# Half of a opens in two half-row parts, and a late turn of a stands one place earlier, in a fused matmul, GELU, matmul kernel

## The chip, the cores and the metric

The kernel runs on one NeuronCore of a Trainium2 chip. The metric is the device time of one execution in microseconds (us). Shown times are medians of several executions; a profile is of one execution, whose own time is given beside its span.

## The reference

```python
m, k, n, p = 1024, 1024, 2048, 1024            # a: m x k, b: k x n, c: n x p, all float32

def reference(a, b, c):
    h = np.matmul(a, b)
    h = 0.5 * h * (1 + np.tanh(np.sqrt(2 / np.pi) * (h + 0.044715 * h ** 3)))
    return np.matmul(h, c).astype(np.float32)
```

## The kernel before

All of the work is laid out by hand: the order in which instructions are written is the order in which each engine takes them, and semaphores that the framework derives from the tiles order the engines against each other. Both matrix products are cut into two by two blocks of 512 rows or columns and use seven block products where that helps; nothing from line 231 on differs in the change, so only the opening is described.

The opening computes the first half of the transposed hidden layer's upper part, `h11`: eight tiles of 128 columns of b (index t) by the first 512 rows of a. Each tile sums over eight slices of 128 of the inner dimension (index k, `KT` = 8, `KH` = 4). A product in this stage is one TensorE matmul of 128 by 512 (`mm0`, L151): the weights are a tile of b's slice k in bf16 (`b_lo`), the moving side is `aT[0][:, k, :]`, the transposed a. The sums lie in PSUM banks: `ps[0]` to `ps[5]` come from the pool `ppool` (six banks), `ps[6]` and `ps[7]` from `tpool` (two banks).

**Loads.** The SP queue loads a's first half as four tiles of 128 full rows (`load_a0`, L70, 512 KB each) and then b's left half slice by slice (`load_b0`, L77, 512 KB each, six buffers). POOL loads the other half of a (`a1`, L181) and then the rest of b, the later slices and c. It starts behind a small copy of b's slice 4 (`gate`, L86), and `a1` takes the same four buffers that `ab` held.

**Turning a.** Each tile mt of a is cast to bf16 in two halves of 512 columns (`cast_a0`: g = 0 on DVE at L103, g = 1 on ACT at L105). Four TensorE transposes turn a half (`turn0`, L113) into a PSUM bank. A copy takes it to `aT[0]` (`copy0`: DVE at L119, ACT at L121). One half covers slices 0 to 3 or 4 to 7. Before the first product of the opening, both halves of tiles 0, 1 and 2 are turned, and the first half of tile 3; the second half of tile 3 is turned amid slice 0 (L156). Each turn writes a bank of its own: two of `tpool` in rotation, and two of `ppool` (`side`) for tile 2. Products of zeros (`warm_up`, L95) fill TensorE between the turns.

**Casting b.** `cast_b0(k)` casts a slice of b to bf16, half on ACT (L130) and half on DVE (L132), one slice ahead of the products.

**Products.** Slices 0 to 3 run over seven tiles, slices 4 to 7 over six; tile 6 then takes its last four slices and tile 7 all eight. Between the two halves of tile 7 stand the first two late turns of a (`turn(0)`, `turn(1)`: eight transposes at L191, a DVE copy at L192 and an ACT copy at L193 each). The other two late turns follow the first half-width product (`mm1_half`, eight products of 128 by 256, L198). GELU on ACT (L169) empties the banks.

Of the kernel before, what the change touches and what calls it, by code (L numbers as in the profile page):

```python
# [9 lines left out]
F32 = mybir.dt.float32  # L10
BF16 = mybir.dt.bfloat16
# [3 lines left out]
AF = mybir.ActivationFunctionType  # L15
# [4 lines left out]
def kernel(ctx, tc, a, b, c, out):  # L20
    nc = tc.nc
    M, K = a.shape
    _, N = b.shape
    _, P = c.shape
    KT = K // 128
    NT = N // 128
    MT = M // 128
    H = 512
    N0 = 6
    W0 = N // 2  # L30
    KH = KT // 2
    NH = NT // 2
    R = range(4)

    av = a.rearrange("(mt p) k -> p mt k", p=128)
    bv = b.rearrange("(kt p) n -> p kt n", p=128)
# [5 lines left out]
    astage = ctx.enter_context(tc.tile_pool(name="astage", bufs=4))  # L42
    abf = ctx.enter_context(tc.tile_pool(name="abf", bufs=4))
    b0stage = ctx.enter_context(tc.tile_pool(name="b0stage", bufs=6))
    opool = ctx.enter_context(tc.tile_pool(name="opool", bufs=4))
    ppool = ctx.enter_context(tc.tile_pool(name="ppool", bufs=6, space=PSUM))
    tpool = ctx.enter_context(tc.tile_pool(name="tpool", bufs=2, space=PSUM))

    warm = consts.tile([128, H], BF16, name="warm")
# [11 lines left out]
                               for g in range(2)] for h in range(2)]  # L61


    a_st, b_st = {}, {}

    def load_a0(mt, parts):
        st = astage.tile([128, K], F32, name="a_st")
        w = K // parts
        for i in range(parts):
            nc.sync.dma_start(out=st[:, ts(i, w)], in_=av[:, mt, ts(i, w)])  # L70
        a_st[mt] = st

    def load_b0(k, parts):
        st = b0stage.tile([128, W0], F32, name="b0_st")
        w = W0 // parts
        for i in range(parts):
            nc.sync.dma_start(out=st[:, ts(i, w)], in_=bv[:, k, ts(i, w)])  # L77
        b_st[k] = st

    gate = consts.tile([128, 1], F32, name="gate")  # L80
    for mt in R:
        load_a0(mt, 1)
    for k in range(KT):
        load_b0(k, 1)

    nc.gpsimd.tensor_copy(gate, b_st[4][:, 0:1])  # L86
    g = consts.tile([128, 1], F32, name="g")
    nc.scalar.activation(g, warm[:, 0:1], AF.Gelu_apprx_tanh)

    side = [ppool.tile([128, 8, 128], BF16, name="ps", tag="ps") for _ in range(2)]  # L90
    ps = [ppool.tile([128, H], F32, name="ps", tag="ps") for _ in range(4)]

    def warm_up(n):
        for _ in range(n):
            nc.tensor.matmul(ps[3], warm[:, 0:128], warm, start=True, stop=True)  # L95

    warm_up(8)
    ab = []

    def cast_a0(mt, g):  # L100
        if g == 0:
            ab.append(abf.tile([128, K], BF16, name="ab1"))
            nc.vector.tensor_copy(ab[mt][:, 0:512], a_st[mt][:, 0:512])  # L103
        else:
            nc.scalar.activation(ab[mt][:, 512:K], a_st[mt][:, 512:K], AF.Copy)  # L105

    def turn0(mt, g):
        if mt == 2:
            pt = side[g]
        else:  # L110
            pt = tpool.tile([128, 8, 128], BF16, name="pt", tag="pt")
        for k in range(4):
            nc.tensor.transpose(pt[:, k, :], ab[mt][:, ts(4 * g + k, 128)], ident)  # L113
        return pt

    def copy0(mt, g, pt):
        dst = aT[0][:, ts(g, 4), ts(mt, 128)]
        if g == 0:
            nc.vector.tensor_copy(dst, pt[:, 0:4, :])  # L119
        else:  # L120
            nc.scalar.activation(dst, pt[:, 0:4, :], AF.Copy)  # L121

    HW = W0 // 2

    def cast_b0(k):
        v = {0: ((HW, W0),), 1: ((0, 256), (256, HW))}.get(k, ((0, HW),))
        a = {0: ((0, 256), (256, HW))}.get(k, ((HW, W0),))
        for i in range(max(len(v), len(a))):
            if i < len(a):
                nc.scalar.activation(b_lo[:, k, slice(*a[i])], b_st[k][:, slice(*a[i])], AF.Copy)  # L130
            if i < len(v):
                nc.vector.tensor_copy(b_lo[:, k, slice(*v[i])], b_st[k][:, slice(*v[i])])  # L132

    for mt in range(3):
        cast_a0(mt, 0)
        cast_a0(mt, 1)
        pt = [turn0(mt, 0), turn0(mt, 1)]
        if mt == 2:
            cast_a0(3, 0)
        copy0(mt, 0, pt[0])  # L140
        copy0(mt, 1, pt[1])
        warm_up((3, 6, 2)[mt])
    copy0(3, 0, turn0(3, 0))
    warm_up(2)
    ps += [ppool.tile([128, H], F32, name="ps", tag="ps") for _ in range(2)]
    cast_b0(0)
    cast_a0(3, 1)

    def mm0(t, ks):
        for k in ks:  # L150
            nc.tensor.matmul(ps[t], b_lo[:, k, ts(t, 128)], aT[0][:, k, :],  # L151
                             start=(k == 0), stop=(k == KT - 1))

    for t in range(N0):
        mm0(t, (0,))
    pt = turn0(3, 1)  # L156
    ps.append(tpool.tile([128, H], F32, name="pt", tag="pt"))
    mm0(6, (0,))
    cast_b0(1)
    copy0(3, 1, pt)  # L160
    ps.append(tpool.tile([128, H], F32, name="pt", tag="pt"))
    for k in range(1, KT):
        if k + 1 < KT:
            cast_b0(k + 1)
        for t in range(N0 + 1 if k < 4 else N0):
            mm0(t, (k,))

    def gelu(dst, src):
        nc.scalar.activation(dst, src, AF.Gelu_apprx_tanh)  # L169

    def bank(w=H):
        return ppool.tile([128, w], F32, name="ps", tag="ps", padded_shape=[128, H])
# [6 lines left out]
    for j in R:  # L179
        st = abf.tile([128, K], BF16, name="ab1")  # L180
# [7 lines left out]
    def turn(j):  # L188
        pt = ppool.tile([128, KT, 128], BF16, name="ps", tag="ps")
        for k in range(KT):  # L190
            nc.tensor.transpose(pt[:, k, :], a1[j][:, ts(k, 128)], ident)  # L191
        nc.vector.tensor_copy(aT[1][:, :, ts(j, 128)], pt)  # L192
        nc.scalar.activation(a22[:, :, ts(j, 128)], aT[1][:, KH:KT, ts(j, 128)], AF.Copy)  # L193

    def mm1_half(t, q):
        p = bank(256)
        for k in range(KT):
            nc.tensor.matmul(p, b_lo[:, k, ts(t, 128)], aT[1][:, k, ts(q, 256)],  # L198
                             start=(k == 0), stop=(k == KT - 1))
        gelu(h21[:, t, ts(q, 256)], p)  # L200
# [5 lines left out]
                             start=(k == 0), stop=(k == KT - 1))  # L206
        gelu(dst, p)

    mm0(6, range(4, KT))
    gelu(h11[:, 6, :], ps[6])  # L210
    mm0(7, range(4))
    turn(0)
    turn(1)
    mm0(7, range(4, KT))
    gelu(h11[:, 7, :], ps[7])
    mm1_half(0, 0)
    turn(2)
    turn(3)
    mm1_half(1, 0)
    mm1_half(2, 0)  # L220
# [77 lines left out]
    for j in R:  # L298
        p = bank()
        prod(p, KH, whole(bx), whole(aT[0]), j)  # L300
        nc.scalar.activation(v2[:, j, :], p, AF.Copy)
    for j in R:
        p = bank()
# [4 lines left out]
    for j in R:  # L308
        p = bank()
# [8 lines left out]
    for j in R:  # L318
        p = bank()
# [10 lines left out]
    for j in R:  # L330
        p = bank()
# [5 lines left out]
    for j in R:  # L337
        p = bank()
# [24 lines left out]
    for j in R:  # L363
        p = bank()
# [29 lines left out]
    for j in R:  # L394
        p = bank()
# [4 lines left out]
    for j in R:  # L400
        p = bank()
# [5 lines left out]
    for j in R:  # L407
        p = bank()
# [8 lines left out]
    for j in R:  # L417
        p = bank()
# [3 lines left out]
    for j in R:  # L422
        p = bank()
        prod(p, NH, halves(s2), whole(c22), j)
        combine(j, 1, p, p5[:, j, :])
    for j in R:
        p = bank()
        prod(p, NH, whole(h22), pairs(t2), j)
        combine(4 + j, 0, p, u3[j])
    for j in range(3):  # L430
        p = bank()
        prod(p, NH, whole(h12), whole(c21), j)
        combine(j, 0, p, p1[:, j, :])
    for q0, w, queue in ((0, 256, nc.sync), (256, 128, nc.scalar), (384, 128, nc.sync)):
        p = bank(w)
# [33 lines left out]
```

## Time and profile before

| What | Value |
|---|---|
| median of 8 runs | 121.01 us (120.39 to 121.19) |
| profiled execution, its own time | 120.5 us |
| its span | 118.7 us |
| TensorE busy with products | 113.9 us (96%) |
| DVE busy | 81.9 us (69%) |
| ACT busy | 46.3 us (39%) |
| POOL busy | 26.6 us (22%) |
| TensorE clock granted, mean | 0.999 |

The span runs from the first to the last instruction; the execution's own time is 1.8 us longer, for what lies around it. Busy time is the union of an engine's instructions; TensorE's is counted with overlapping, pipelined matmuls, so 96% does not say that each of them runs at its best rate. In lines of the timeline the first number is the start in us, the second the time from the first start to the last end of a merged group, then engine, line, operation, what it writes and reads, its shape and how many; in brackets stands the engine's idle time before it and what ended that.

### The profile page before, as it was taken

What the parts mean: (1) busy time and instruction counts of PE and PEld (TensorE: products, weight loads), DVE (VectorE), ACT (ScalarE), POOL (GpSimd) and SP (SyncE); (2) the same over time, 40 slices, a digit from 0 to 9 for tenths busy, and PEclk for the clock granted to TensorE, in tenths of its full rate; (3) what the DMA queues carried; (4) which work ended last, traced back from release to release, by engine and by line L of the source; (5) the groups of instructions that cost most, each with busy time, mean ns of one, the idle gap of its engine ahead of it and who ended that gap; (6) DMA issues with size and microseconds to landing.
All of it is one profiled execution on the core that took longest, in us unless ns stands there. A gap on an engine that the chain in (4) does not pass through costs nothing.

```text
span 118.7 us, 1596 instructions
## 1 busy us (share of the span) xinstructions
PE 113.9 (96%) x583; PEld 76.4 (64%) x589; DVE 81.9 (69%) x112; ACT 46.3 (39%) x78; POOL 26.6 (22%) x39
## 2 busy tenths in 40 slices
PE   5999999999999999999999999999999999999990
PEld 2554444469744445888887447888888888886460
DVE  0344322048999917999999999995789992824450
ACT  5366744987332474306369998430000000000000
POOL 2000069752200000086305229100006500000000
PEclk9999999999999999999999999999999999999999
DMA  3999999999999999949999999999997999954434
GB/s 115 407 384 282 420 420 223 180 359 386 213 211 203 206 206 375 359 113 247 250 235 202 190 196 200 182 204 148 141 163 159 243 266 342 344 197 160 175 116 151
DMA packets 13543, 28.41 MB, mean 239 GB/s; under 512 B 992, under 2 KB 5472, under 8 KB 13536
## 3 DMA queue, kind: packets, MB, share of 16 engines
q0 software_dynamic: 9216, 17.83, 73.0%
q1 hardware_dynamic: 4176, 10.42, 23.5%
q8 instruction: 4, 0.07, 0.2%
q10 hardware_dynamic: 144, 0.07, 0.2%
q14 instruction: 3, 0.02, 0.1%
HBM read 20.97 MB, written 4.19 MB: 212 GB/s over the span
## 4 chain that ended last, share of the span: by engine, by line
PE 94%; DVE 2%; ACT 1%; issue 1%
PE ps L267 63%; PE ps L151 9%; PE ps L205 7%; PE ps L198 5%; PE ps L95 4%; PE pt L151 2%; PE pt L113 1%; PE ps L191 1%; DVE aT L192 1%; ACT aT L121 1%; ACT ab L105 0%; PE ps L113 0%; DVE aT L119 0%; DVE ot L438 0%; DVE warm L50 0%
## 5 line engine op out<-in xcount | busy, mean ns | idle before, releaser
L267 PE MATMUL ps<-t,s 128*128 128x512 f32 x64 | 14.9, 392 | 0.0
L267 PE MATMUL ps<-c,h 128*128 128x512 bf16 (+2 forms) x78 | 14.1, 336 | 0.1
L267 PEld LDWEIGHTS ps<-t,s 128*128 128x128 f32 x64 | 12.0, 188 | 2.6
L275 DVE TENSOR_TENSOR ot<-ps,v 128x512 f32<-128x512 f32 x16 | 10.5, 695 | 3.1 <-PE ps L267 3.1
L169 ACT ACTIVATE h<-ot 128x512 bf16<-128x512 f32 (+1 forms) x16 | 9.4, 624 | 5.9 <-DVE ot L275 5.9
L267 PE MATMUL ps<-t,h 128*128 128x512 f32 x48 | 11.7, 389 | 0.0
L267 PEld LDWEIGHTS <-h 128*128 128x128 bf16 x80 | 7.1, 98 | 7.0 <-issue 0.5
L169 ACT ACTIVATE h<-ps 128x512 bf16<-128x512 f32 (+2 forms) x17 | 8.3, 528 | 8.2 <-PE ps L205 5.9
L383 DVE TENSOR_TENSOR ot<-ps,p 128x512 f32<-128x512 f32 x11 | 7.5, 689 | 5.5 <-PE ps L267 3.1
L151 PE MATMUL ps<-aT,b_lo 128*128 128x512 bf16 x46 | 11.1, 379 | 0.2
L151 PEld LDWEIGHTS <-b_lo 128*128 128x128 bf16 x64 | 6.1, 98 | 7.6 <-DVE b_lo L132 0.6
L267 PEld LDWEIGHTS ps<-t,h 128*128 128x128 f32 x48 | 9.0, 188 | 1.9
L205 PE MATMUL ps<-aT,b_lo 128*128 128x512 bf16 x39 | 8.7, 379 | 0.1
L95 PE MATMUL ps<-warm 128*128 128x512 bf16 x21 | 7.3, 485 | 1.2 <-DVE warm L50 1.2
L132 DVE CAST b_lo<-b_st 128x512 bf16<-128x512 f32 (+1 forms) x9 | 3.5, 396 | 6.3 <-DMA b_st<-in_b_dram 6.3
L267 PE MATMUL ps<-as,bt 128*128 128x512 f32 x32 | 7.7, 396 | 0.0
L285 POOL DMA_DIRECT2D c<-in_c_dram x8 | 6.4, 838 | 5.6 <-DMA b<-in_b_dram 3.9
L267 PE MATMUL ps<-c,s 128*128 128x512 f32 x32 | 7.4, 389 | 0.0
L267 PE MATMUL ps<-as,b 128*128 128x512 f32 x32 | 7.4, 389 | 0.0
L267 PE MATMUL ps<-aT,bx 128*128 128x512 bf16 x31 | 7.0, 379 | 0.1
L416 POOL DMA_DIRECT2D t<-c x4 | 3.5, 1041 | 15.5 <-PE ps L267 14.5
L267 PEld LDWEIGHTS ps<-as,bt 128*128 128x128 f32 x32 | 6.0, 188 | 1.4
(71 smaller groups left out, 171.5 us busy)
## 6 DMA issues: line engine op xcount, KB each, us to landing
b_st<-in_b_dram SPq DMA_DIRECT2D x8, 512.0 KB, 9.0
out_dram<-ot SPq DMA_DIRECT2D x15, 256.0 KB, 2.1
c<-in_c_dram POOLq DMA_DIRECT2D x6, 512.0 KB, 18.1
t<-c POOLq DMA_DIRECT2D x6, 512.0 KB, 6.6
a_st<-in_a_dram SPq DMA_DIRECT2D x4, 512.0 KB, 4.6
b<-in_b_dram POOLq DMA_DIRECT2D x2, 1024.0 KB, 10.4
c<-in_c_dram POOLq DMA_DIRECT2D x2, 1024.0 KB, 21.0
t<-t POOLq DMA_DIRECT2D x4, 512.0 KB, 8.6
```

Of the source, the lines that this page charges most:

```text
L95: nc.tensor.matmul(ps[3], warm[:, 0:128], warm, start=True, stop=True)
L113: nc.tensor.transpose(pt[:, k, :], ab[mt][:, ts(4 * g + k, 128)], ident)
L132: nc.vector.tensor_copy(b_lo[:, k, slice(*v[i])], b_st[k][:, slice(*v[i])])
L151: nc.tensor.matmul(ps[t], b_lo[:, k, ts(t, 128)], aT[0][:, k, :], start=(k == 0), stop=(k == KT - 1))
L169: nc.scalar.activation(dst, src, AF.Gelu_apprx_tanh)
L198: nc.tensor.matmul(p, b_lo[:, k, ts(t, 128)], aT[1][:, k, ts(q, 256)], start=(k == 0), stop=(k == KT - 1))
L205: nc.tensor.matmul(p, b_lo[:, k, ts(t, 128)], aT[h][:, k, :], start=(k == 0), stop=(k == KT - 1))
L267: nc.tensor.matmul(p, lhs(t)[:, ts(j, 128)], rhs(t)[:, q], start=(t == 0), stop=(t == n - 1))
L275: tt(ot, p, u, op=ADD)
L285: nc.gpsimd.dma_start(out=dst[:, t:t + 4, :], in_=cv[:, r * NH + t:r * NH + t + 4, ts(q, H)])
L383: tt(ot, p, u, op=ADD)
L416: nc.gpsimd.dma_start(out=t2[i], in_=c21[:, P2[i], :], accum_op=ADD)
```

## The change

The four tiles of a's first half are now loaded in half rows: 256 KB each for slices 0 to 3 first, then b's slices 0 to 3, then the other half rows, then b's slices 4 to 7. Only the first halves of the four tiles are cast, turned and copied ahead of the first product, each into the bank of a later sum (`ps[0]` to `ps[3]`), with the work divided anew between DVE and ACT. The second halves are cast behind the casts of slice 3, those of tiles 2 and 3 later between the copies; tile 0's is turned amid slice 3, after its fourth product, and those of tiles 1, 2 and 3 between slice 3 and slice 4. All four second-half turns write `ps[7]`, which is cut into two halves that they use in turn. Slices 4 to 7 then run over seven tiles like the first four, so tile 6 is done with them and tile 7 alone follows. Warm-up products go into `ps[5]`, and are 8 + 2 + 2 + 2 + 4. Last, `turn(2)` stands ahead of the GELU of tile 7 and of the first half-width product, where it stood behind it.

```diff
-    def load_a0(mt, parts):
-        st = astage.tile([128, K], F32, name="a_st")
...
+    def load_a0(g):
+        for mt in R:
+            nc.sync.dma_start(out=a_st[mt][:, ts(g, H)], in_=av[:, mt, ts(g, H)])
...
-    for mt in R:
-        load_a0(mt, 1)
-    for k in range(KT):
-        load_b0(k, 1)
+    for g in range(2):
+        load_a0(g)
+        for k in range(g * KH, g * KH + KH):
+            load_b0(k)
...
-    side = [ppool.tile([128, 8, 128], BF16, name="ps", tag="ps") for _ in range(2)]
-    ps = [ppool.tile([128, H], F32, name="ps", tag="ps") for _ in range(4)]
+    ps = [ppool.tile([128, H], F32, name="ps", tag="ps") for _ in range(N0)]
+    ps += [tpool.tile([128, H], F32, name="pt", tag="pt") for _ in range(2)]
...
+    def turned(mt, g):
         if g == 0:
+            return ps[mt][:, :].bitcast(BF16)[:, 0:512].rearrange("p (k m) -> p k m", k=4)
+        return ps[7][:, :].bitcast(BF16)[:, ts(mt % 2, 512)].rearrange("p (k m) -> p k m", k=4)
...
-    for mt in range(3):
-        cast_a0(mt, 0)
-        cast_a0(mt, 1)
-        pt = [turn0(mt, 0), turn0(mt, 1)]
-        if mt == 2:
-            cast_a0(3, 0)
-        copy0(mt, 0, pt[0])
-        copy0(mt, 1, pt[1])
-        warm_up((3, 6, 2)[mt])
-    copy0(3, 0, turn0(3, 0))
+    cast_a0(0, 0, True)
+    turn0(0, 0)
     warm_up(2)
+    cast_a0(1, 0, False)
+    copy0(0, 0, True)
+    turn0(1, 0)
+    warm_up(2)
+    cast_a0(2, 0, True)
+    copy0(1, 0, False)
+    turn0(2, 0)
+    warm_up(2)
+    cast_a0(3, 0, True)
+    copy0(2, 0, False)
+    turn0(3, 0)
+    warm_up(4)
+    copy0(3, 0, True)
     cast_b0(0)
-    cast_a0(3, 1)
...
-    for t in range(N0):
-        mm0(t, (0,))
-    pt = turn0(3, 1)
-    ps.append(tpool.tile([128, H], F32, name="pt", tag="pt"))
-    mm0(6, (0,))
-    cast_b0(1)
-    copy0(3, 1, pt)
-    ps.append(tpool.tile([128, H], F32, name="pt", tag="pt"))
-    for k in range(1, KT):
-        if k + 1 < KT:
+    for k in range(KH):
+        if k + 1 < KH:
             cast_b0(k + 1)
-        for t in range(N0 + 1 if k < 4 else N0):
+        else:
+            cast_a0(0, 1, True)
+            cast_a0(1, 1, False)
+        for t in range(7):
+            mm0(t, (k,))
+            if k + 1 == KH and t == 3:
+                turn0(0, 1)
+                copy0(0, 1, True)
+    turn0(1, 1)
+    copy0(1, 1, False)
+    cast_a0(2, 1, True)
+    turn0(2, 1)
+    cast_a0(3, 1, True)
+    copy0(2, 1, False)
+    turn0(3, 1)
+    copy0(3, 1, True)
+    for k in range(KH, KT):
+        cast_b0(k)
+        for t in range(7):
             mm0(t, (k,))
...
-    mm0(6, range(4, KT))
     gelu(h11[:, 6, :], ps[6])
-    mm0(7, range(4))
+    mm0(7, range(KH))
     turn(0)
     turn(1)
-    mm0(7, range(4, KT))
+    mm0(7, range(KH, KT))
+    turn(2)
     gelu(h11[:, 7, :], ps[7])
     mm1_half(0, 0)
-    turn(2)
     turn(3)
```

The last argument of `cast_a0` and `copy0` is the engine: True is DVE, False ACT.

More of the change, by code (lines that the diff above doesn't have):

```diff
@@ L61, with load_b0 @@
                                for g in range(2)] for h in range(2)]
-    a_st, b_st = {}, {}
-    def load_a0(mt, parts):
-        st = astage.tile([128, K], F32, name="a_st")
[L68 to L78, printed above, removed]
+    a_st = [astage.tile([128, K], F32, name="a_st") for _ in R]
+    b_st = {}
+    def load_a0(g):
+        for mt in R:
+            nc.sync.dma_start(out=a_st[mt][:, ts(g, H)], in_=av[:, mt, ts(g, H)])
+    def load_b0(k):
+        b_st[k] = b0stage.tile([128, W0], F32, name="b0_st")
+        nc.sync.dma_start(out=b_st[k], in_=bv[:, k, 0:W0])
     gate = consts.tile([128, 1], F32, name="gate")
-    for mt in R:
-        load_a0(mt, 1)
-    for k in range(KT):
-        load_b0(k, 1)
+    for g in range(2):
+        load_a0(g)
+        for k in range(g * KH, g * KH + KH):
+            load_b0(k)
     nc.gpsimd.tensor_copy(gate, b_st[4][:, 0:1])
@@ L88, with cast_a0, copy0 @@
     nc.scalar.activation(g, warm[:, 0:1], AF.Gelu_apprx_tanh)
-    side = [ppool.tile([128, 8, 128], BF16, name="ps", tag="ps") for _ in range(2)]
-    ps = [ppool.tile([128, H], F32, name="ps", tag="ps") for _ in range(4)]
+    ps = [ppool.tile([128, H], F32, name="ps", tag="ps") for _ in range(N0)]
+    ps += [tpool.tile([128, H], F32, name="pt", tag="pt") for _ in range(2)]
     def warm_up(n):
         for _ in range(n):
-            nc.tensor.matmul(ps[3], warm[:, 0:128], warm, start=True, stop=True)
+            nc.tensor.matmul(ps[5], warm[:, 0:128], warm, start=True, stop=True)
     warm_up(8)
-    ab = []
-    def cast_a0(mt, g):
+    ab = [abf.tile([128, K], BF16, name="ab1") for _ in R]
+    def turned(mt, g):
         if g == 0:
-            ab.append(abf.tile([128, K], BF16, name="ab1"))
-            nc.vector.tensor_copy(ab[mt][:, 0:512], a_st[mt][:, 0:512])
+            return ps[mt][:, :].bitcast(BF16)[:, 0:512].rearrange("p (k m) -> p k m", k=4)
+        return ps[7][:, :].bitcast(BF16)[:, ts(mt % 2, 512)].rearrange("p (k m) -> p k m", k=4)
+    def cast_a0(mt, g, vector):
+        if vector:
+            nc.vector.tensor_copy(ab[mt][:, ts(g, H)], a_st[mt][:, ts(g, H)])
         else:
-            nc.scalar.activation(ab[mt][:, 512:K], a_st[mt][:, 512:K], AF.Copy)
+            nc.scalar.activation(ab[mt][:, ts(g, H)], a_st[mt][:, ts(g, H)], AF.Copy)
     def turn0(mt, g):
-        if mt == 2:
-            pt = side[g]
-        else:
-            pt = tpool.tile([128, 8, 128], BF16, name="pt", tag="pt")
+        pt = turned(mt, g)
         for k in range(4):
             nc.tensor.transpose(pt[:, k, :], ab[mt][:, ts(4 * g + k, 128)], ident)
-        return pt
-    def copy0(mt, g, pt):
+    def copy0(mt, g, vector):
         dst = aT[0][:, ts(g, 4), ts(mt, 128)]
-        if g == 0:
-            nc.vector.tensor_copy(dst, pt[:, 0:4, :])
+        if vector:
+            nc.vector.tensor_copy(dst, turned(mt, g))
         else:
-            nc.scalar.activation(dst, pt[:, 0:4, :], AF.Copy)
+            nc.scalar.activation(dst, turned(mt, g), AF.Copy)
     HW = W0 // 2
@@ L132, in cast_b0 @@
                 nc.vector.tensor_copy(b_lo[:, k, slice(*v[i])], b_st[k][:, slice(*v[i])])
-    for mt in range(3):
-        cast_a0(mt, 0)
-        cast_a0(mt, 1)
-        pt = [turn0(mt, 0), turn0(mt, 1)]
-        if mt == 2:
-            cast_a0(3, 0)
-        copy0(mt, 0, pt[0])
-        copy0(mt, 1, pt[1])
-        warm_up((3, 6, 2)[mt])
-    copy0(3, 0, turn0(3, 0))
-    warm_up(2)
-    ps += [ppool.tile([128, H], F32, name="ps", tag="ps") for _ in range(2)]
+    cast_a0(0, 0, True)
+    turn0(0, 0)
+    warm_up(2)
+    cast_a0(1, 0, False)
[11 more added lines that the diff above has]
+    copy0(3, 0, True)
     cast_b0(0)
-    cast_a0(3, 1)
     def mm0(t, ks):
```

## The prediction

> **What bounds the kernel now.** I read the chain of waits first, then the timeline up to 28 us in order of time, because the change touches nothing later.
>
> ```profile
> ## 4 chain that ended last, share of the span: by engine, by line
> PE 94%; DVE 2%; ACT 1%; issue 1%
> PE ps L267 63%; PE ps L151 9%; PE ps L205 7%; PE ps L198 5%; PE ps L95 4%; PE pt L151 2%; PE pt L113 1%; PE ps L191 1%; DVE aT L192 1%; ACT aT L121 1%; ACT ab L105 0%; PE ps L113 0%; DVE aT L119 0%; DVE ot L438 0%; DVE warm L50 0%
> ```
>
> TensorE carries the end nearly throughout: a microsecond of TensorE idleness in the opening moves the end by a microsecond, unless a later idle takes it back. So I need two things: when the first product (L151) starts, and how densely TensorE runs from there.
>
> ```profile
> 4.00 0.43 DVE L103 CAST ab<-a_st 128x512 bf16<-128x512 f32 x1 [2.87 <-DMA a_st<-in_a_dram]
> 6.85 0.40 PE L113 MATMUL pt<-ident,ab 128*128 128x128 bf16 x4 [0.17 <-ACT ab L105]
> 7.28 0.60 ACT L121 ACTIVATE aT<-pt 128x512 bf16<-128x512 bf16 x1 [0.49 <-PE pt L113]
> 8.04 0.43 DVE L103 CAST ab<-a_st 128x512 bf16<-128x512 f32 x1 [0.56 <-DMA a_st<-in_a_dram]
> 9.25 0.39 PE L113 MATMUL pt<-ident,ab 128*128 128x128 bf16 x4
> 9.68 0.43 DVE L119 COPY aT<-pt 128x512 bf16<-128x512 bf16 x1 [0.45 <-PE pt L113]
> 10.15 1.46 PE L151 MATMUL ps<-aT,b_lo 128*128 128x512 bf16 x5
> 11.70 0.50 DVE L132 CAST b_lo<-b_st 128x256 bf16<-128x256 f32 x2 [1.27 <-DMA b_st<-in_b_dram]
> ```
>
> Rows of a land from 4.0 to 8.0 us, 1.3 us apart; the last is cast, turned, copied, and L151 begins at 10.15. A turn (four transposes) until the end of its copy takes 0.86 us on DVE (9.25 to 10.11) and 1.03 us on ACT (6.85 to 7.88). Both serve as prices below.
>
> ```profile
> 12.05 1.47 PE L151 MATMUL ps<-aT,b_lo 128*128 128x512 bf16 x6
> 16.60 5.34 PE L151 MATMUL ps<-aT,b_lo 128*128 128x512 bf16 x23
> 21.78 1.89 PE L151 MATMUL pt<-aT,b_lo 128*128 128x512 bf16 x8
> 24.40 1.03 PE L151 MATMUL pt<-aT,b_lo 128*128 128x512 bf16 x4
> 25.50 1.05 PE L198 MATMUL ps<-aT,b_lo 128*128 128x256 bf16 x8
> 27.27 4.53 PE L198 MATMUL ps<-aT,b_lo 128*128 128x256 bf16 x40
> ```
>
> From 12.05 the products follow at 0.2155 us each (24 from 16.60 to 21.78); L198's half-width ones take 0.108, and a transpose 0.056 (16 of L191 between 23.50 and 24.40). Idle from 10.15 to 27.27 is about 0.4 us: 0.17 before 12.05, where b's second slice is late, and 0.24 before 25.50, where L198 waits for L192 (the six products from 10.15 to the turn at 11.45 fill 1.30 without a gap; one record is missing). I take 27.27, the start of half-width tile 1, as the milestone.
>
> **What the Trainium skill says.** "PSUM — Partial Sum Buffer", section on bank collisions, says to guard PSUM by bank and not by address, since two engines may not touch a bank's partitions together. The kernel before, with a bank for each turn, shows no such wait; the new code puts four turns into one bank. "TensorE: Matmul & The Clock Gate", Part 1, says that full clock comes only after a busy window of about 3.4 us that runs freely, and is lost after an idle one. The trace agrees on the first half: L95's first eight products fill 3.4 us from 1.19, 0.43 each, and six from 7.08 start 0.215 apart. No run here shows the loss. "DMA: Bandwidth & Descriptors", Anatomy, gives about 2 us fixed to a transfer; the first 512 KB of a, issued at 0.74, landed at 4.00, of which 1.28 is data at the spacing of later slices, so 1.98: agreed.
>
> **Part 1: half rows first.** SP issues four 256 KB half rows of a, b's slices 0 to 3, the other four half rows, then b 4 to 7: 16 issues for 12, each about 0.45 us, less than the 0.64 us of data of a half. Four more fixed costs in a pipelined queue cost nothing. The queue's 2 KB packets of output take 86 ns where the 4 KB ones of a take 159, so a half lands every 0.69 us: at about 3.4, 4.1, 4.8, 5.5, and b's slice 0 at 6.8 to 7.0. Ahead of b slice 4 stand the same 4.5 MB as before, so that slice and POOL's gate (L86), behind which all loads of a's second half are queued, stay near 15.6 us at the latest.
>
> With half the turns, TensorE's own order sets the start: eight warm-ups to 4.58 as now; four cold transposes to 5.00, two cold warm-ups to 5.86, then three turns (0.28 in the first case, else 0.22) with two warm-ups (0.43) between, ending at 7.46, and four warm-ups (0.86): 8.32. The last opening copy runs 7.66 to 8.09 and b's first cast on ACT 7.5 to 7.9, both under those warm-ups. So the first product starts at S = 8.32 against 10.15, **1.8 us earlier**. Before, DMA hid part of a late clock rise; in the new order all is TensorE, so S can be 8.3 to 9.5. I take 8.35 against the profiled rise.
>
> **Part 2: the other half, amid the products.** Slices 0 to 2 take 3 x 7 x 0.2155 = 4.53, four products of slice 3 take 0.86; the first second-half turn starts at T = S + 5.39 = 13.7. By then its half row has landed (about 11.5; 12.5 if the slow delivery of b's slice 1, 2.4 us instead of 1.28, recurs). Casts of the half rows on DVE and ACT stand behind casts of slice 3; DVE has 0.9 us of work for every 1.5 of TensorE, so they hide.
>
> The four turns then share bank ps[7], and the built program's list of waits has each turn waiting for the copy of the one before: turn 1 for DVE's copy 0, turn 2 for ACT's copy 1, turn 3 for ACT's copy 2; the last copy, on DVE, comes ahead of DVE's cast of b slice 4, for which the first product of slice 4 waits. Counted from T:
> - copy 0 (DVE) ends 0.86; three products of slice 3 cover TensorE to 0.87; turn 1 starts 0.90 (0.04 for a wait).
> - its copy on ACT ends 0.90 + 1.03 = 1.93; turn 2 starts 1.98, copy ends 3.01; turn 3 starts 3.06, DVE's copy ends 3.92.
> - DVE's cast of slice 4, which overlaps by 0.09 (9.68, then 10.02 in the trace), ends 4.26; slice 4 starts at 4.30.
>
> So TensorE stands from 0.87 to 4.30, 3.43 us, with 12 transposes (0.67) of its own: **2.76 us idle**, where the kernel before had one turn, 0.22 us, with six products around it. Nothing covers this: the remaining products all need all four quarters of aT, and tile 7 has no free bank until the turns are done. ACT's half of slice 4 is cast by T + 3.7, hidden.
>
> **Part 3: after it.** Slices 4 to 7 at seven tiles: 28 x 0.2155 = 6.03; tile 7's first four 0.86; 16 transposes 0.90; its last four 0.86; turn(2), now here, 0.45; half-width tile 0 0.86; turn(3) 0.45. The milestone is at T + 4.30 + 10.41 = S + 20.10 = 28.45, against 27.27: **+1.18 us**. Moving turn(2) ahead adds no work; it covers L198's wait of 0.24, already in this count. On ACT the copy of turn(2) now stands before tile 7's gelu; the banks that later work needs are freed by gelus ahead of it, and the 0.6 us hide. Its load lands at about 23.9 now and would be needed at 26.7. POOL's four loads reuse the buffers of ab and wait for the turns; the last waits for turn 3 at T + 3.3 = 17.0, while now it goes out at about 18.1: no delay. SP's late slices 6 and 7 may share the engines with POOL's loads about a microsecond earlier; slice 7 would land by 20 and is needed at 22.6.
>
> **What takes it back later?** Nothing that I find: DVE's sums L244 to L254 shift with it and have 4.8 us in hand:
>
> ```profile
> 39.78 2.36 DVE L254 TENSOR_TENSOR bt<-b,b 128x1024 fp32r<-128x1024 f32 x2
> 46.99 7.65 PE L267 MATMUL ps<-as,bt 128*128 128x512 f32 x32
> ```
>
> **Sum.** -1.80 (start) -0.41 (old idles) +2.76 (new idle) +0.67 (12 transposes more amid the products) is +1.22, or +1.18 by the milestone: +1.2. The profiled execution took 120.5 (span 118.7); it would be 121.7. The median, 121.01, lies 0.5 above it, which I read as a later clock rise or a slower slice of b; to the median the sum gives 122.2, and 0.1 is added for the new start's exposure to the clock: **122.3 us**.
>
> **Unknown costs.** The clock phase at the start: between nothing and +1.2 on S, against a part of that in the kernel before; I take +0.1. The slow slice of b: its recurrence costs nothing (b's slice 1 is needed at 9.8 and would land by 9.5), and if it held the kernel before in typical runs, its removal gives up to 0.5 back. The ACT copies of a shared bank: 0.57 to 0.63 each, plus or minus 0.1 over two.
>
> **Rivals.**
> - *The clock falls back* (8%). The 3.43 us hold only transposes, about one window of the skill's 3.4. If it counts as idle, products go at 0.43 for a window, 8 to 16 of them: +1.7 to 3.4. The time would be about 124.2. Against it: three bursts of work fall inside, and the window must align.
> - *The start gains less* (14%). b's slice 0 lands late or the rise comes at 8 us: S near 9.2, the time 123.0.
> - *A slow slice held the median run before* (14%): the new order is free of it; +0.7, 121.7.
> - *The turns do not wait for each other* (4%, faster). If the chain of copies at ps[7] were short, with turns back to back and both engines copying at once, slice 4 would start at T + 2.55 instead of T + 4.30, and the sum be 1.2 - 1.75 = -0.55: 120.5. It decides from T + 3.1 downward, where the gain of the start outweighs the gap. Against it stand the program's waits named above and the 1.03 us of each ACT turn.
> - *No difference to be seen* (6%): half of that shortening and a slow slice gone.
>
> **How the numbers follow.** The forecast itself has 54% and its own range is 121.9 to 122.7. The late start, slow slice and clock add above and below: 121.4 to 123.7 leaves out the faster and equal cases and half of the clock's. Within 0.3% (0.36 us), about what a measurement here can tell from no change: faster 0.04, same 0.06, slower 0.90.
>
> **What would show it.** Right: the first product (line 149 in the new file) near 8.3 to 8.5; a wall of about 3.4 us between slices 3 and 4, near 14.6 to 18.0, with three bursts of four transposes, each released by a copy of the turn before; then no idle before the half-width tiles and the same work after them, 1.2 us later. Wrong: the first product after 9, turns released by their own casts only, or 0.43 us spacing after the gap.

## The result and the profile after

The changed kernel took **124.16 us** in the median (123.22 to 125.77, 11 executions) against 121.06 for the kernel before on the same chip: a ratio of 1.0242, 95% interval 1.0217 to 1.0266, or +2.9 us (the two medians lie 3.1 apart). Forecast were 122.3 us and a range up to 123.7. The direction was right, the size less than half of what came. The profiled execution took 123.22 us with a span of 121.4, which is 2.7 above the span before. Executions that stood apart by over 1.5% are left out of ratios, not out of medians.

The chain of waits of the changed kernel, on its page:

```profile
## 4 chain that ended last, share of the span: by engine, by line
PE 87%; DMA 5%; ACT 1%; SPq 1%; DVE 1%; issue 1%
PE ps L274 62%; PE ps L149 9%; PE ps L213 7%; DMA b_st<-in_b_dram 5%; PE ps L206 4%; PE pt L149 3%; PE ps L199 1%; SPq L69 1%; ACT aT L116 1%; PE pt L109 1%; DVE b_lo L127 1%; ACT b_lo L125 0%; DVE aT L114 0%; DVE ot L445 0%
```

TensorE's share fell from 94 to 87%. A transfer of b, which was not on the chain before, now carries 5% of the span: at the start the chain runs through SP's issues and b's slice 0, where it ran through warm-up products and turns.

From the timeline up to the first product (start, duration, engine, line, what; in brackets the idle time before and what ended it):

```profile
3.39 0.43 DVE L102 CAST ab<-a_st 128x512 bf16<-128x512 f32 x1 [2.25 <-DMA a_st<-in_a_dram]
5.07 0.63 ACT L104 ACTIVATE ab<-a_st 128x512 bf16<-128x512 f32 x1 [2.83 <-DMA a_st<-in_a_dram]
5.74 0.43 DVE L102 CAST ab<-a_st 128x512 bf16<-128x512 f32 x1 [0.27 <-DMA a_st<-in_a_dram]
6.40 0.43 DVE L102 CAST ab<-a_st 128x512 bf16<-128x512 f32 x1 [0.24 <-DMA a_st<-in_a_dram]
7.30 1.03 PE L89 MATMUL ps<-warm 128*128 128x512 bf16 x4
9.01 0.43 DVE L127 CAST b_lo<-b_st 128x512 bf16<-128x512 f32 x1 [1.09 <-DMA b_st<-in_b_dram]
9.48 1.47 PE L149 MATMUL ps<-aT,b_lo 128*128 128x512 bf16 x6 [1.16 <-DVE b_lo L127]
```

The first half row came at 3.4 as forecast. The second came 1.67 us behind it and not 0.69; b's slice 0 landed at 8.98, 2.6 us behind the last half row and not 1.3. TensorE's own order held: its last warm-ups ended at 8.33, as forecast. Then it stood for 1.16 us until slice 0 was cast, so the first product stands at 9.48, where 8.35 was forecast. In e2, e4 and e5 below, which load in the same way, it stands at 9.97, 9.67 and 9.80.

The gap between slices 3 and 4:

```profile
14.89 0.39 PE L109 MATMUL pt<-ident,ab 128*128 128x128 bf16 x4
15.31 0.42 DVE L114 COPY aT<-pt 128x512 bf16<-128x512 bf16 x1 [1.24 <-PE pt L109]
15.79 0.38 PE L109 MATMUL pt<-ident,ab 128*128 128x128 bf16 x4
16.21 0.60 ACT L116 ACTIVATE aT<-pt 128x512 bf16<-128x512 bf16 x1 [1.26 <-PE pt L109]
16.86 0.38 PE L109 MATMUL pt<-ident,ab 128*128 128x128 bf16 x4 [0.69 <-ACT aT L116]
17.28 0.60 ACT L116 ACTIVATE aT<-pt 128x512 bf16<-128x512 bf16 x1 [0.47 <-PE pt L109]
17.93 0.38 PE L109 MATMUL pt<-ident,ab 128*128 128x128 bf16 x4 [0.69 <-ACT aT L116]
18.43 0.42 DVE L114 COPY aT<-pt 128x512 bf16<-128x512 bf16 x1 [2.02 <-ACT b_lo L125]
19.24 1.47 PE L149 MATMUL ps<-aT,b_lo 128*128 128x512 bf16 x6 [0.93 <-DVE b_lo L127]
```

Each turn starts when the copy of the one before has ended; where ACT copies, a link takes 1.07 us. From the first turn to slice 4 it is 4.35 us (4.30 forecast). After it TensorE is dense again, and the half-width tile 1 starts at 29.68, 20.20 us behind the first product (20.10 forecast) and 2.41 us later than in the kernel before:

```profile
27.92 0.61 PE L199 MATMUL ps<-ident,ab 128*128 128x128 bf16 x8
28.36 1.04 PE L206 MATMUL ps<-aT,b_lo 128*128 128x256 bf16 x8
29.24 0.61 PE L199 MATMUL ps<-ident,ab 128*128 128x128 bf16 x8
29.68 4.53 PE L206 MATMUL ps<-aT,b_lo 128*128 128x256 bf16 x40
```

The last TensorE work of the program also ends 2.40 us later (118.12 against 115.72 on the chain in order of time), so between the milestone and the last product nothing is lost or won. In the profiled execution the opening holds these 2.4 us: +1.18 as forecast, +1.13 for the later first product, +0.10 for the rest. The other 0.3 us of the longer span lie behind the last product, where the program closes (3.0 us before, 3.3 now).

There is more in the other executions. Twelve with a recorded clock fall into two groups: six with a mean granted TensorE clock of 0.995 to 1.0 (median 123.65 us) and six with 0.981 to 0.986 (median 125.3 us). In the four comparisons of the experiments that list the kernel before run by run (27, 11, 27 and 27 executions of it), its lowest is 0.996.

### The profile page after: what moved, and what is told of

Its sections match the earlier page's. It is cut to its first block, busy times and chain, and to the rows that moved or that the text cites. A ratio compares the mean times of both kernels' runs of the same rounds, so it can differ in the third digit from the quotient of the medians.

```text
span 121.4 us, 1596 instructions
## 1 busy us (share of the span) xinstructions
PE 112.8 (93%) x580; PEld 75.8 (62%) x586; DVE 82.7 (68%) x114; ACT 45.0 (37%) x76; POOL 26.4 (22%) x39
## 4 chain that ended last, share of the span: by engine, by line
PE 87%; DMA 5%; ACT 1%; SPq 1%; DVE 1%; issue 1%
PE ps L274 62%; PE ps L149 9%; PE ps L213 7%; DMA b_st<-in_b_dram 5%; PE ps L206 4%; PE pt L149 3%; PE ps L199 1%; SPq L69 1%; ACT aT L116 1%; PE pt L109 1%; DVE b_lo L127 1%; ACT b_lo L125 0%; DVE aT L114 0%; DVE ot L445 0%
## 5 line engine op out<-in xcount | busy, mean ns | idle before, releaser
L149 PE MATMUL ps<-aT,b_lo 128*128 128x512 bf16 x46 | 11.6, 379 | 2.2 <-DVE b_lo L127 2.1
L213 PE MATMUL ps<-aT,b_lo 128*128 128x512 bf16 x39 | 8.7, 379 | 0.1
L89 PE MATMUL ps<-warm 128*128 128x512 bf16 x18 | 6.4, 491 | 1.2 <-DVE warm L50 1.2
L200 DVE COPY aT<-ps 128x1024 bf16<-128x1024 bf16 x4 | 2.7, 689 | 6.7 <-PE ps L199 6.7
```

The costliest lines, as they stand in the source:

```text
L89: nc.tensor.matmul(ps[5], warm[:, 0:128], warm, start=True, stop=True)
L213: nc.tensor.matmul(p, b_lo[:, k, ts(t, 128)], aT[h][:, k, :], start=(k == 0), stop=(k == KT - 1))
```

## The experiments

The edits of a group are against the changed kernel where nothing else is said. Most kernels here have four executions only, so the reading rests on their profiles and clocks more than on their medians. The kernel before had medians of 120.95 to 121.22 us in these comparisons, so times of different groups can be set side by side to about 0.3 us.

### Which part costs what: the late turn, the chain, the loads

**e1: only the late turn, on the kernel before.**

```diff
     mm0(7, range(4, KT))
+    turn(2)
     gelu(h11[:, 7, :], ps[7])
     mm1_half(0, 0)
-    turn(2)
     turn(3)
```

> Only the last edit, on the kernel before: turn(2) ahead of the GELU of tile 7 and of half-width tile 0. My theory: it covers the 0.24 us for which L198 waited before 25.50, so 0.2 us faster than before (120.85 against 121.06), and none of the loss of the whole change comes from it. Rival: the DVE copy of turn(2) or its load comes late and delays half-width tile 0 or 1, 0.3 us or more slower.

Measured: 121.02 us against 121.22, ratio 0.998 (0.9959 to 1.0). From its timeline of TensorE:

```profile
24.22 1.03 PE L151 MATMUL pt<-aT,b_lo 128*128 128x512 bf16 x4
25.09 0.61 PE L191 MATMUL ps<-ident,ab 128*128 128x128 bf16 x8
25.53 1.04 PE L198 MATMUL ps<-aT,b_lo 128*128 128x256 bf16 x8
```

The wait ahead of L198 is gone, as forecast: the turn and the first half-width product follow each other with no idle time. The gain, 0.2 us, is what the wait had cost, at the edge of what can be told.

**e2: all four second-half copies on DVE, casts of tiles 1 to 3 on ACT.**

```diff
-    copy0(1, 1, False)
-    cast_a0(2, 1, True)
+    copy0(1, 1, True)
+    cast_a0(2, 1, False)
...
-    cast_a0(3, 1, True)
-    copy0(2, 1, False)
+    cast_a0(3, 1, False)
+    copy0(2, 1, True)
```

> The changed kernel with all four second-half copies on DVE and the casts of tiles 1 to 3 on ACT. My theory: the gap between slices 3 and 4 is the chain of turn and copy at one bank; two copies become 0.17 us shorter each, so the gap shrinks from 3.48 to 3.14 us and the time falls by 0.34 us from the changed kernel's. If a TensorE clock that falls back in part of the executions comes from the length of that gap, the executions with a mean granted clock near 0.982 become fewer and the median falls by up to 1 us more. Rival: the gap is set by the late half rows or by slice 4 of b; then nothing changes (within 0.1).

```profile
16.34 0.38 PE L149 MATMUL pt<-aT,b_lo 128*128 128x512 bf16 x1
16.59 0.38 PE L109 MATMUL pt<-ident,ab 128*128 128x128 bf16 x4
17.49 0.38 PE L109 MATMUL pt<-ident,ab 128*128 128x128 bf16 x4 [0.52 <-DVE aT L114]
18.39 0.38 PE L109 MATMUL pt<-ident,ab 128*128 128x128 bf16 x4 [0.51 <-DVE aT L114]
19.62 1.47 PE L149 MATMUL ps<-aT,b_lo 128*128 128x512 bf16 x6 [0.85 <-DVE b_lo L127]
```

Links of 0.90 in place of 1.07, a gap of 3.06 us (19.62 less 16.34 and the 0.22 of that product) where the changed kernel has 3.48. The median was 123.3, ratio 1.0159 (1.0112 to 1.0207), and one of four executions had a low clock (0.986). The gap follows the length of the copies.

**e3: the loads of the kernel before, all else as changed.**

```diff
-    for g in range(2):
-        load_a0(g)
-        for k in range(g * KH, g * KH + KH):
-            load_b0(k)
+    for mt in R:
+        nc.sync.dma_start(out=a_st[mt], in_=av[:, mt, :])
+    for k in range(KT):
+        load_b0(k)
```

> The changed kernel with the loads of the kernel before: four full row tiles of a, then b's slices 0 to 7; everything after the loads as in the changed kernel. My theory: the half-row loads bring the first product forward only from 9.75 to 9.48 us, since b's slice 0 landed at 8.98 against 9.26; here b's slice 1 lands at 11.68 as in the kernel before and holds slice 1 until 12.05, so the time is 0.8 to 1.1 us above the changed kernel's, and the gap between slices 3 and 4 stays near 3.4 us although all of a has landed by 8.0. Rival: the gap comes from the late half rows; then it closes to under 1 us and the time falls below the changed kernel's.

```profile
16.99 0.38 PE L149 MATMUL pt<-aT,b_lo 128*128 128x512 bf16 x1
18.30 0.38 PE L109 MATMUL pt<-ident,ab 128*128 128x128 bf16 x4 [0.69 <-ACT aT L116]
19.37 0.38 PE L109 MATMUL pt<-ident,ab 128*128 128x128 bf16 x4 [0.69 <-ACT aT L116]
20.68 1.47 PE L149 MATMUL ps<-aT,b_lo 128*128 128x512 bf16 x6 [0.93 <-DVE b_lo L127]
```

All of a had landed by 8.9 us and b's slice 4 by 15.9, before the gap begins, and the gap is 3.47 us: neither the late half rows nor slice 4 make it. With e2, this shows that the chain of turns and copies sets the gap. The first product came at 10.69, later than the 9.75 expected, since a's third tile landed at 7.64 and not 6.7. Median 125.84, ratio 1.0361 (1.0307 to 1.0416); three of four executions had a clock of 0.986, and the one without took 124.34, 0.7 above the changed kernel's 123.65.

**e4: the chain starts earlier, amid slice 3.**

```diff
-            if k + 1 == KH and t == 3:
+            if k + 1 == KH and t == 0:
                 turn0(0, 1)
                 copy0(0, 1, True)
+            if k + 1 == KH and t == 4:
+                turn0(1, 1)
...
+            if k + 1 == KH and t == 5:
+                turn0(2, 1)
```

> The changed kernel with the second-half turns amid slice 3: tile 0's after its first product, tile 1's after the fifth, tile 2's after the sixth, tile 3's after the last. The chain of four turns and copies at one bank starts 0.65 us earlier and is otherwise the same. My theory: slice 4 starts 0.65 us earlier and the time falls by 0.65 us; with products between the turns the clock does not fall back, and the low granted clocks near 0.982 vanish, so the median falls by about 1.2 us. Rival: the half rows, which land from 13.6 to 15.6 us, hold the chain; then the gain is under 0.2 us.

```profile
14.83 0.40 PE L109 MATMUL pt<-ident,ab 128*128 128x128 bf16 x4
15.06 1.03 PE L149 MATMUL ps<-aT,b_lo 128*128 128x512 bf16 x4
15.93 0.39 PE L109 MATMUL pt<-ident,ab 128*128 128x128 bf16 x4
```

Nothing was gained: slice 4 began 9.71 us behind the first product where the changed kernel has 9.76. The rival named the right size and a part of the cause. The second half rows landed from 14.32 to 16.34 us in this profile, and the first turn waited 0.15 us for its cast, until 14.83. Slice 1 had come 0.2 us late, and the second turn stood behind four products where the changed kernel has three, another 0.2 us; its cast and the first copy, done at 15.64 and 15.68, would have let it start 0.2 us sooner at most. Median 123.43, ratio 1.0227 (1.017 to 1.0284). One of four executions had a low clock (0.981) although products stood between the turns.

### The clock

**e5: products of zeros in the gap.**

```diff
     turn0(1, 1)
+    zeros(3)        # nc.tensor.matmul(ps[t], warm[:, 0:128], warm, start=False, stop=False)
...
     turn0(2, 1)
+    zeros(3)
...
     turn0(3, 1)
+    zeros(4)
```

> The changed kernel with ten products of zero weights in the gap between slices 3 and 4: three behind the turns of tiles 1 and 2 each, four behind tile 3's. They add zero to open sums, so the result stays, and take 0.65 or 0.86 us in places where TensorE waits 0.69 or 0.93: the gap keeps its length. My theory: in about half of the changed kernel's executions the TensorE clock is lost for one window after this gap; with the gap filled no execution has a mean granted clock under 0.99, and the times lie between 123.0 and 124.0, where the changed kernel's spread to 125.8. Rival: the low clocks have another cause (the waits for b's slice 0 near 8 us, or chance); then they come as often as before and the median stays near 124.2.

```profile
18.93 1.03 PE L165 MATMUL ps<-warm 128*128 128x512 bf16 x4
20.15 1.47 PE L149 MATMUL ps<-aT,b_lo 128*128 128x512 bf16 x6 [0.20 <-DVE b_lo L127]
```

All six executions had a clock of 0.997 or more, with a stretch between slices 3 and 4 that is no shorter (3.6 us). Median 123.56 us, ratio 1.0198 (1.0156 to 1.0239). In the eight kernels here whose gap is not filled (the changed one, e2, e3, e6, e7, e8, e10, and e4 with a few products in it), 16 of 40 executions had 0.986 or less; at that rate none in six would come by chance about once in twenty times (an estimate, 0.6 to the sixth power). Times reached 124.44, above the 124.0 expected: the profiled one, 124.12, had its first product at 9.80 and waited for slice 1 besides. So what is left of the spread is not the low clock; in this one profile it lay in the loads.

The profile of e6 below caught such an execution. Its busy time by stretch (columns: stretch in us and its length, busy time and count of TensorE, of its weight loads, of DVE, ACT and POOL, then granted TensorE clock, DMA share, GB/s) and the line of slice 4:

```profile
12.20:15.50 3.30, 3.25 (x19) 1.62 (x20) 1.35 (x4) 1.32 (x3) 0.00 (x0) 1.00 1.06 415
15.50:18.40 2.90, 1.14 (x13) 0.76 (x11) 0.88 (x3) 2.02 (x4) 1.28 (x3) 0.99 1.03 420
18.40:21.70 3.30, 2.77 (x7) 1.01 (x8) 1.68 (x5) 1.47 (x3) 3.30 (x6) 0.50 1.08 259
21.70:25.00 3.30, 3.30 (x15) 1.46 (x15) 0.00 (x0) 0.00 (x0) 2.54 (x4) 0.99 1.09 210
```

```profile
18.93 2.74 PE L151 MATMUL ps<-aT,b_lo 128*128 128x512 bf16 x6 [0.93 <-DVE b_lo L129]
```

TensorE is busy for 1.14 of 2.90 us in the gap, then runs at half clock for 3.4 us; slice 4's six products take 2.74 us and not 1.47. In the clock's record the half rate runs from 18.37 for 3.41 us. Half of that is 1.7 us, which is how far apart the two groups of the changed kernel lie (125.3 and 123.65). This is the loss for which the prediction had no run. In the Trainium skill, "TensorE: Matmul & The Clock Gate", Part 1, gives a window of about 3.4 us for the loss as for the gain, and calls it free-running. The 3.41 us agree, and a free-running window would explain why the same gap is punished in some executions only; that explanation is argued, not shown. The page speaks of an idle window; here the transposes in the gap did not prevent the loss.

### The start

**e6: an early small read of b.**

```diff
+    touch = consts.tile([128, 2, 8], F32, name="touch")
+    nc.scalar.dma_start(out=touch, in_=bv[:, 0:2, 0:8])
```

> The changed kernel with a small early read of b, 32 bytes of each of its first 256 rows, issued from ACT's queue at the start. In all runs so far the first 0.5 MB or so of b came at half speed for about 2.3 us, at 8.1 to 10.6 us with b behind a (kernel before) and at 6.5 to 8.9 us with b behind half of a. Theory first touch: what is slow is the first access to b's rows, and the early read takes the cost; slice 0 then lands near 7.8 instead of 9.0 and the time falls by about 1 us. Rival: it is not the first access; slice 0 lands at 9.0 or later (the small reads cost queue time) and the time is the same or worse.

Slice 0 landed at 8.40 us, 2.1 us behind the last half row (6.26), so the slow stretch stayed (the kernels without this read that load in the same way have 2.1 to 2.6). Median 124.36, ratio 1.0203 (1.0129 to 1.0278), with three of four executions at a low clock. First touch, in this form, falls.

**e7: b's slices in the order 3, 2, 1, 0, 7, 6, 5, 4.** Casts and sums follow the same order; the edit of the loads:

```diff
-        for k in range(g * KH, g * KH + KH):
+        for k in range(g * KH + KH - 1, g * KH - 1, -1):
             load_b0(k)
```

> The changed kernel with b's slices loaded and summed in the order 3, 2, 1, 0 and then 7, 6, 5, 4 (the sums take the slices in that order). If the slow delivery belongs to the rows of slices 0 and 1, then slice 3, now first, lands near 7.7 us, the first product starts near 8.4 and the slow stretch comes with slices 1 and 0; the time falls by up to 1 us. Rival: it belongs to whatever of b is read first, or to the time: then slice 3 lands near 9.0, and nothing else changes.

Slice 3, now first, landed at 8.48, 2.3 us behind the last half row (6.14), and the first product came at 8.97. The slow stretch goes with what of b is read early, not with certain rows. Median 123.64, ratio 1.0196 (1.0138 to 1.0255).

**e8: a's half rows in two transfers per half**, into other buffers.

```diff
-        for mt in R:
-            nc.sync.dma_start(out=a_st[mt][:, ts(g, H)], in_=av[:, mt, ts(g, H)])
+        for i in range(2):
+            nc.sync.dma_start(out=a_pr[i][:, :, ts(g, H)], in_=av[:, 2 * i:2 * i + 2, ts(g, H)])
```

> The changed kernel with a's half rows in two transfers of 512 KB for two tiles each instead of four of 256 KB (other buffers, 12 issues on SP's queue instead of 16). In the changed kernel the second transfer landed 1.67 us behind the first instead of 0.69, with half the engines' packets missing from 3.0 to 4.0 us. My theory: that stall comes from the number of small transfers at the start; here the first half of a has landed by about 5.3 us instead of 6.4, b's slice 0 by 8.0 to 8.3, and the time falls by 0.5 to 0.8 us. Rival: it comes from the 2 KB packets themselves; then the first half of a lands at 6.4 again.

```profile
5.03 0.43 DVE L101 CAST ab<-a_pr 128x512 bf16<-128x512 f32 x1 [3.89 <-DMA a_pr<-in_a_dram]
7.75 0.71 ACT L124 ACTIVATE b_lo<-b_st 128x256 bf16<-128x256 f32 x2
8.57 1.46 PE L148 MATMUL ps<-aT,b_lo 128*128 128x512 bf16 x6
```

The first half of a was in at 6.30, no earlier than the changed kernel's 6.37, so the rival was right on that: fewer transfers do not cure the slow start of the half rows. But slice 0 landed at 7.61, only 1.3 us behind it, and the slow stretch fell on slice 1 (9.77), where it hardly hurts. The first product stands at 8.57, behind warm-ups as in the forecast. The gap is unchanged (3.47 us, slice 4 at 18.57). This is the forecast's case on the chip: executions of 122.25 and 122.40 us, against 122.3. Two more took 123.66 and 123.89; the last had a clock of 0.986, and what made the other long is not on record. Median 123.03, ratio 1.0144 (1.0085 to 1.0203).

**e10: b's slice 0 from ACT's queue, beside a's half rows.**

```diff
-        nc.sync.dma_start(out=b_st[k], in_=bv[:, k, 0:W0])
+        (nc.scalar if k == 0 else nc.sync).dma_start(out=b_st[k], in_=bv[:, k, 0:W0])
```

with `load_b0(0)` called first.

> The changed kernel with b's slice 0 issued from ACT's queue at the start, beside a's first half rows on SP's, all else the same. In every run so far the first MB of b's slices came at about half speed, whichever slices they were. Theory 1: the slow packets wait and leave the engines free for another queue's; slice 0 then lands by 7.5 us with a's half rows by 7.0, slice 1 by 9.0 (10.4 in the changed kernel), the first product starts near 8.5 and the time falls by about 1 us. Theory 2: the slow stretch binds the engines or the memory; then a's half rows are held up with it, slice 1 lands at 10 us or later, and the time falls by under 0.4 us.

Slice 0 landed at 6.15 us, but a's half rows at 5.97, 6.76, 7.44 and 8.11, and the first product stood at 9.88. From 2 to 5 us both queues together moved 180, 268 and 293 KB in the three microseconds, a's queue only 76 to 94 KB of it in each; from 6 to 8 us it was 419 KB a microsecond. Theory 2 holds for a, and slice 1 at 9.39 lies between the two. Median 123.38, ratio 1.0193 (1.0141 to 1.0245). Behind slice 0, slices of b came 1.3 us apart with no further slow stretch, but the wait had moved to a. What makes the slow stretch stays open: rows, first touch by a small read, and the number of transfers were tried and are not it. Which slice it delays does go with the transfers ahead of b. In the six profiles with four transfers of 256 KB there, b's first slice landed 2.1 to 2.6 us behind a's last part; in the five with transfers of 512 KB (the kernel before, e3, e8, e9, e11) it landed 1.25 to 1.31 behind it, and b's second slice 1.9 to 2.4 us behind the first.

### What the findings allow

**e9: two links in place of four**, on e8: tiles 0 and 1 are turned together behind slice 2, tiles 2 and 3 behind slice 3.

```diff
+    def copy_pair(i):
+        nc.vector.tensor_copy(aT[0][:, KH:KT, ts(i, 256)], pair7())
...
+        if k == 2:
+            turn0(0, 1)
+            turn0(1, 1)
+            copy_pair(0)
+            cast_b0(3)
+    turn0(2, 1)
+    turn0(3, 1)
+    copy_pair(1)
```

The half rows of tiles 0 and 1 load ahead of b's slice 3, and ACT casts the first-needed half of slice 4.

> The kernel with half rows in two transfers per half, changed so that the chain at the shared bank has two links instead of four: tiles 0 and 1 are turned together behind slice 2 (their second half rows load ahead of b's slice 3), tiles 2 and 3 together behind slice 3, and one DVE copy of 128 by 1024 (0.69 us) takes each pair; ACT casts the half of b's slice 4 that is needed first. My theory: slice 4 starts near 17.0 to 17.3 us instead of 18.6, no stretch of 3.4 us without products is left and no granted clock falls under 0.99, so the time is 1.3 to 1.6 us under that kernel's clean 122.3: 120.7 to 121.0, level with the kernel before (121.2) or up to 0.4% faster. Rival: what is lost was not the chain but the half rows' arrival; then slice 4 starts at 18 us or later and the time stays above 122.

Median 121.72, ratio 1.0049 (1.0027 to 1.0072); no clock below 0.997. Better than e8 by over a microsecond, short of the 121.0 expected. Two things in its profile:

```profile
5.55 0.61 PE L121 MATMUL ps<-ident,ab 128*128 128x128 bf16 x4 [0.76 <-DVE ab L114]
8.51 1.06 PE L95 MATMUL ps<-warm 128*128 128x512 bf16 x2
11.02 1.46 PE L161 MATMUL ps<-aT,b_lo 128*128 128x512 bf16 x6
17.29 1.47 PE L161 MATMUL ps<-aT,b_lo 128*128 128x512 bf16 x6 [1.12 <-DVE b_lo L139]
```

TensorE had nothing to do ahead of 5.55, and two warm-ups still took 1.06 us at 8.51 where they take 0.59 at full clock, so the first product waited until 11.02. In the clock's record full rate begins at 10.53 us. The mean clock of this execution is nevertheless given as 1.0: the figure leaves out what lies ahead of the record's first entry, so a late rise does not show in it. And slice 3 waited for its cast on DVE, which I had put behind the pair's copy.

**e11: both mended, on e9.**

```diff
-    warm_up(8)
+    warm_up(11)
...
-            copy_pair(0)
             cast_b0(3)
+            copy_pair(0)
```

> The kernel with two pairs of turns and two edits: b's slice 3 is cast on DVE ahead of the first pair's copy instead of behind it, and the first run of warm-up products is 11 instead of 8. Theory: in the profile of the last kernel TensorE had nothing to do from 4.6 to 5.5 us and full clock came only at 10.53, which made the first product start at 11.02; 11 warm-ups (about 1.3 us more at 0.43 each) reach to 5.9 and the clock comes by 6 us in all executions, so the times near 123.5 vanish. Slice 3 then waits for its transfer (13.5 us) and not for the copy, which takes up to 1 us off the clean 121.6: 120.6 to 121.2, level with the kernel before (120.95). Rival: the late rise is chance; then a third of the executions still lies 2 us above the rest.

```profile
8.76 1.46 PE L161 MATMUL ps<-aT,b_lo 128*128 128x512 bf16 x6
14.23 1.47 PE L161 MATMUL ps<-aT,b_lo 128*128 128x512 bf16 x6 [0.32 <-DVE b_lo L139]
17.14 1.46 PE L161 MATMUL ps<-aT,b_lo 128*128 128x512 bf16 x6 [0.78 <-DVE aT L110]
27.57 2.67 PE L220 MATMUL ps<-aT,b_lo 128*128 128x256 bf16 x23
```

Median **120.77 us** against 121.14, ratio 0.9981 (0.9964 to 0.9998), all 22 executions between 120.50 and 121.20. Eight of e9's 22 had lain at 123.1 to 124.0; none does here, and in the profile full clock is on record from 5.55 us. The two edits were not run apart. That the warm-ups ended the late times is argued from the start, which they alone can change: the other edit acts only from 12 us on.

The median is clearly under the changed kernel's and 0.2% under that of the kernel before, at the edge of what can be told and no more than the late turn alone gives (e1). In the profiles the products start 1.4 us sooner (8.76 against 10.15), yet half-width tile 1 starts 0.3 us later (27.57 against 27.27; the kernel before was profiled in one of its faster executions). What half rows win at the start is given back, because slice 4 needs the second half rows and its own transfer: the last of these rows landed at 15.05 us, and slice 4, at the end of the same 4.5 MB, at 16.34 (15.54 in the kernel before).

## Why the prediction was wrong in size

**The gap, right.** Four turns on one bank: 4.35 us from the first turn to slice 4 against 4.30, and e2 and e3 show that the copies make it, not the loads.

**Everything behind the gap, right.** The milestone lies 20.20 us behind the first product (20.10 forecast); nothing later took any of it back; the late turn is worth 0.2 us (e1).

**The start, wrong: the term "S = 8.35".** The step that failed is b's slice 0 "at 6.8 to 7.0". It took the steady spacing of the queue, 0.69 us for a half row and 1.28 for a slice, for its first megabyte and a half. Measured were 6.37 for the last half row (5.5 forecast) and 8.98 for slice 0, so S was 9.48. TensorE's order, on which S was summed, was right (8.33); the load that was to hide behind it came 2 us late and set S in its place. The trace of before had shown the slow stretch, but I read it as a property of slice 1, by which it ended, and so wrote that its recurrence "costs nothing". It comes with the early reads of b, whichever rows those are (e7), and behind four half-row transfers it delayed slice 0, for which everything waits. Behind two transfers of twice the size (e8) slice 0 was on time, the start came at 8.57, and two executions took 122.25 and 122.40. Of the sixteen parts in which slice 0 lands, fourteen were in by 7.63 us in the changed kernel and the last two at 8.46 and 8.99; why those two is open. The mis-sized term is 1.1 us.

**The clock, wrong in its chance.** The rival was named with the right mechanism and a price of 1.7 to 3.4 us; it measures 1.7. But it was given 8%, on the ground that three bursts of transposes fall inside, and it came in six of twelve executions. At the median it adds about 0.5 us: 124.16 against 123.65 for executions without it. Between medians 1.3 us were forecast and 3.1 came. Start and clock make 1.6 of the 1.8 that were missing; the last 0.2 is not traced.

**The start's rival** (S near 9.2, 123.0 us) was the nearest to the truth: with S at 9.48 it gives 123.4 (122.3 and 1.13), and executions at full clock have 123.65. The range, up to 123.7, held the late start alone and only half of the clock's cases, so not the two together.

**A smaller miss.** POOL's gate was to open at 15.6 and opened at 16.97, since b's slice 4 landed at 16.91. It cost nothing: the first late turn stands at 26.16, its load landed at 21.8.

## What to carry to other kernels

Splitting the first load let the work begin sooner, but it paid nothing, since what the second product stage needs did not come sooner: the bytes ahead of that stage had not changed. Turns that share a bank cost a full turn and copy each, about a microsecond here (0.90 with a DVE copy, 1.07 with an ACT copy), so put several into one copy (0.69 us for two tiles) or give them banks of their own. And a stretch without products in front of dense matmul work, here 3.1 to 3.6 us, can have a price beyond its length (1.7 us), to be counted with the chance that it is hit (16 of 40 executions).

## What the hardware showed unexpectedly

- An early stretch of b comes slowly wherever b stands in the queue: in the changed kernel 588 KB from 6.5 to 9.0 us, in the kernel before 584 KB from 8.1 to 10.6 us, where about 1,000 KB is the later rate. Packets of 4 KB took 241 and 261 ns there in the mean, and 159 in most of the rest. Which slice of b is late for it went with the size of the transfers ahead (256 or 512 KB).
- Half rows at the very start of the program stall once (174 KB from 3.0 to 4.0 us in the changed kernel, 416 KB in full rows in the kernel before), while the second halves run at 200 KB in each half microsecond from the first on.
- Gaps of 3.1 to 3.6 us with 12 transposes in them went with a low clock in 15 of 36 executions. In the one profile that caught it, the TensorE clock fell to half for 3.41 us although TensorE had been busy for 1.14 of 2.90 us. With ten products of zeros in the gap none of six executions was hit.
- In e9, whose profile has a hole of 0.76 us in the warm-up work near 5 us and full clock only at 10.53, eight of 22 executions were about 2 us longer; with three more warm-up products and one cast moved, all 22 were alike. That hole alone does not decide: e8's profile has one of 1.10 us, with full clock on record from 3.91.
